# Closing products of a compressed attention branch: high and low parts of two heads stacked over 128 rows

## The chip, the cores and the metric

The kernel runs on one core of one Trainium2 chip. The metric is the device time of one execution in microseconds. The kernel before took 806.31 us, the median of 3 runs (806.19 to 806.38).

## What is computed

One layer of a decoder trunk on 512 tokens of 1024 features, in float32: a normalised input is projected once to queries, keys, values and gates; three attention branches are mixed by gates; a gated short convolution is merged with them; and a feed-forward block with a squared ReLU ends the layer. The change lies in the first of the three branches, attention over compressed keys. Cut to that:

```python
kc = rms_norm(compress(k_c, cmp_pos_k, w_cmp_k), k_norm_g[0])   # 31 compressed keys, 2 groups
vc = compress(v_c, cmp_pos_v, w_cmp_v)                          # and their values
s_c = einsum('bsgrd,bcgd->bgrsc', q, kc) * SCALE - slopes * dist_c
p_c = masked_softmax(s_c, dist_c >= 0)
o_cmp = einsum('bgrsc,bcgd->bsgrd', p_c, vc)
...
o_nsa = g[:, :, 0] * o_cmp + g[:, :, 1] * o_slc + g[:, :, 2] * o_win
```

There are 8 query heads of 64 features in 2 groups (g) of 4 (r); the heads of a group share keys and values. `o_slc` and `o_win` are the two other branches, over selected blocks and over a window, which for 512 tokens are two softmaxes over all earlier tokens.

## The kernel before

**Numbers in two parts.** Float32 operands are split into a high part, which the engine's fast float32 format holds, and a low part, the rest. ACT (ScalarE) writes the high part with a copy, DVE (VectorE) the low part with a subtraction. A product of two matrices is then high by high, high by low and low by high, added in PSUM (`mm3`, L228 to L232). Weights stream from memory in chunks of 128 x 1024 or less (`Weights`): a DMA on SP's queue (L63), ACT's copy to `w_hi` (L87), DVE's subtraction to `w_lo` (L89). A chunk is split one tile ahead of the products that read it.

**Order of the work.** The program writes the order of each engine's instructions out by hand. The outer loop of the stretch that matters is the convolution's (L759): for each of 8 column blocks three tiles of 24 products each (`tile_t`). After every three products `slot` is called; it issues what is due: steps of a background copy of weight sums by DMA (`tick`), short follow-up work put off by some slots (`later`), and one item of a list, `items`, which holds the whole attention, spread evenly over these slots. So attention work sits between the products of the convolution's projections, and each engine executes in the order of issue.

**The attention items.** A unit is a head and one of two branches; 16 units follow each other, two to a head. For unit u the rounds hold: scores for 4 (or 3) token blocks (`u_scores`, L640), each followed on DVE by a bias and maximum (L648), on ACT by the exponential (L652) and on GpSimd (POOL) by the normalisation (L668); transposes of the probabilities of the unit before in three groups (`u_trans`, L687), split by ACT (L692) and DVE (L693) into `pt`; products of the transposed probabilities of the unit before that with V (`u_pv`, L708 and L711), added up in one PSUM tile `pv`. The transposes of L687 and those of L618 take turns in two PSUM buffers (`ps_tr`); the scores have three buffers (`ps_sc`), and `pv` has one.

**The compressed branch** enters `pv` at the end of each head. Its steps:

- `cmp_v` (L477) makes the compressed values, 64 rows (2 groups of 32) by 64 features, splits them into `vcn` (L480, L481) and copies them into `VC` four times each, at rows 0, 32, 64 and 96 (L489, L491), so that each head finds a copy on the rows on which its probabilities lie.
- `cmp_scores` (L580), once for each of the 4 token blocks, writes the scores of the 8 heads side by side (L585), 2 x 32 columns each, adds the distances and forms the softmax in `pcs` (L595 to L610), 32 columns a head in the order of heads, with the slopes of that order from a constant table and the gates of the branch (L609).
- `cmp_pt` (L615), called for g = 0 and g = 1 in two items right after each other and once in the kernel, transposes four heads of one group at once (L618): 128 rows, 32 for each head, by 512 tokens. ACT copies them to the high tile of `pct[g]` (L623), DVE subtracts into the low one (L624).
- `u_fin` (L715), at the end of each head, has two products. The first is over the head's 32 rows of the low part with the high part of the values (64 columns of weights, L722), the second over the 32 rows of the high part with high and low parts of the values (128 columns, L723). ACT and DVE then add the two halves of `pv` into the head's output `oT` (L725, L726).

The same split of one transposed tile in two halves of 64 rows is done for the query heads in `q_item` (L426): two heads are transposed at once, and for each of them ACT copies its 64 rows (L435) and DVE subtracts (L436).

Of the kernel before, what the change touches and what calls it, by code (L numbers as in the profile page):

```python
# [6 lines left out]
F32 = mybir.dt.float32  # L7
F32R = mybir.dt.float32r
AF = mybir.ActivationFunctionType
ALU = mybir.AluOpType  # L10
# [3 lines left out]
P = 128  # L14
S = 512
DM = 1024
NH = 8
HD = 64
# [86 lines left out]
def layer(tc, flat, sizes, x, cst, wck, wcv, g1, g2, out):  # L105
    nc = tc.nc
    top = ExitStack()

    def pool(name, bufs=1, psum=False, side=None, dram=False):
        kw = dict(name=name, bufs=bufs, reuse_waits="tile")  # L110
        if psum:
            kw["space"] = PSUM
        if dram:
            kw["space"] = bass.MemoryType.DRAM
        if side:
            kw["side"] = side
        es = ExitStack()
        p = es.enter_context(tc.tile_pool(**kw))
        return p, es.close
# [48 lines left out]
    ident = cp.tile([P, P], F32, name="ident")  # L168
# [87 lines left out]
    for c in range(NT):  # L256
        ps = ps_acc.tile([P, 512], F32, name="acc", tag="acc")
        for kp in range(4):
            hi, lo = W.get(kp)
# [16 lines left out]
    for c in range(NT):  # L276
        v = q_sb[:, c, :].rearrange("p (h d) -> p h d", d=HD)
# [67 lines left out]
    def later(k, fn):  # L345
        due.append((pos[0] + k, fn))
# [14 lines left out]
    def tile_t(ci, rhs, nko, psp, tag="acc"):  # L361

        ps = psp.tile([P, S], F32, name="acc", tag=tag)
        tile_t_into(ps, ci, rhs, nko)
        return ps
# [42 lines left out]
    ps = tile_t(ci, (xh, xl), NKO, ps_t)  # L408
# [6 lines left out]
    gates = cp.tile([P, NT, 24], F32, name="gates")  # L415
# [4 lines left out]
    QS = [qkv.tile([P, S], F32R, name=f"QS_{h}") for h in range(NH)]  # L420
# [38 lines left out]
    vcn = pre.tile([64, 2, HD], F32R, name="vcn")  # L459
    kc_ss = pre.tile([64, 1], F32, name="kc_ss")  # L460
    KC = qkv.tile([P, 2, 2, 32], F32R, name="KC")
    VC = qkv.tile([P, 2, 2, HD], F32R, name="VC")

    def compress(ps, nm, w):
        for l in range(16):
            src = KAB[nm + "ab"[l // 8]][:, l % 8, :, :].rearrange("p g c -> p (g c)")
            nc.tensor.matmul(ps, src, w[:, l, :], start=(l == 0), stop=(l == 15))
# [9 lines left out]
    def cmp_v():  # L477
        ps = ps_tr.tile([P, S], F32, name="ptr", tag="tr")
        compress(ps[:64, :HD], "v", wcv_t)
        nc.scalar.activation(vcn[:, 0, :], ps[:64, :HD], AF.Copy)  # L480
        nc.vector.tensor_tensor(  # L481
            vcn[:, 1, :], ps[:64, :HD], vcn[:, 0, :].bitcast(F32), ALU.subtract
        )
        for g in range(2):
            for r in range(4):
                dst = VC[32 * r : 32 * r + 32, g, :, :]
                src = vcn[32 * g : 32 * g + 32, :, :].bitcast(F32)
                if r % 2:
                    nc.vector.tensor_copy(dst, src)  # L489
                else:  # L490
                    nc.scalar.activation(dst, src, AF.Copy)  # L491

    def cmp_kt():
        pt = ps_tr.tile([P, 4, P], F32, name="ptr", tag="tr")
# [2 lines left out]
        src = pt[:, 0, :64].rearrange("p (g c) -> p g c", g=2)  # L497
        nc.scalar.activation(KC[:, :, 0, :], src, AF.Copy, scale=sc)
        nc.vector.scalar_tensor_tensor(
            KC[:, :, 1, :], src, sc, KC[:, :, 0, :].bitcast(F32), op0=ALU.mult, op1=ALU.subtract  # L500
        )
# [30 lines left out]
    for c in range(NT):  # L532
        r = k_ss[:, c, :].unsqueeze(2).to_broadcast([P, 4, HD])
        nc.vector.tensor_tensor(kn[:, c, :, 1, :], kn[:, c, :, 0, :], r, ALU.mult)
        nc.gpsimd.tensor_tensor(kn[:, c, :, 0, :], kn[:, c, :, 0, :], r, ALU.mult)
    ps = tile_t(ci, (xh, xl), NKO, ps_t)
# [3 lines left out]
    for i in range(4):  # L540
        items.append((p0 + 18 + 2 * i, lambda i=i: k_item(i)))
    items.append(kt)
    items.append((p0 + 29, cmp_v))

    acc = kv_gemm(ci)
# [14 lines left out]
    ps_pv, close_ps_pv = pool("ps_pv", 1, psum=True, side="left")  # L560
    ap, close_ap = pool("att")
    pcs = [ap.tile([P, NH, 32], F32, name=f"pc{c}") for c in range(NT)]
    pct = [[ap.tile([P, S], F32R, name=f"pct{g}{i}") for i in range(2)] for g in range(2)]
    pbuf = [
        [ap.tile([P, P * (c + 1)], F32, name=f"p{b}_{c}") for c in range(1, NT)] for b in range(2)
    ]
# [13 lines left out]
    def cmp_scores(c):  # L580
        t = slice(c * P, (c + 1) * P)
        ps = ps_sc.tile([P, NH, 2, 32], F32, name="scc", tag="sc")
        for h in range(NH):
            g = h // 4
            nc.tensor.matmul(  # L585
                ps[:, h, :, :], QS[h][:, t], KC[:, g, :, :].rearrange("p a c -> p (a c)"),
                start=True, stop=True,
            )
        pc = pcs[c]
        s = cst_s[:, c, :]  # L590
        dc = cs[:, C_DC + 32 * c : C_DC + 32 * c + 32].unsqueeze(1).to_broadcast([P, NH, 32])
        mk = cs[:, C_MK + 32 * c : C_MK + 32 * c + 32].unsqueeze(1).to_broadcast([P, NH, 32])
        sl = cs[:, C_SL : C_SL + NH].unsqueeze(2).to_broadcast([P, NH, 32])
        sb = s.unsqueeze(2).to_broadcast([P, NH, 32])
        nc.vector.tensor_tensor(pc, ps[:, :, 0, :], dc, ALU.add)  # L595
        nc.vector.tensor_tensor(pc, ps[:, :, 1, :], pc, ALU.add)
        nc.vector.tensor_reduce(s, pc, AX.X, ALU.max)
        nc.gpsimd.tensor_tensor(pc, pc, sb, ALU.subtract)
        nc.gpsimd.tensor_tensor(pc, pc, sl, ALU.mult)

        def second():
            nc.scalar.activation(pc, pc, AF.Exp)
            nc.gpsimd.tensor_tensor(pc, pc, mk, ALU.mult)

        def third():
            nc.vector.tensor_reduce(s, pc, AX.X, ALU.add)
            nc.vector.tensor_scalar(s, s, 1.0e-30, None, op0=ALU.max)
            nc.vector.reciprocal(s, s)
            nc.vector.tensor_tensor(s, s, gates[:, c, 0:NH], ALU.mult)  # L609
            nc.gpsimd.tensor_tensor(pc, pc, sb, ALU.mult)  # L610

        later(3, second)
        later(6, third)

    def cmp_pt(g):  # L615
        pt = ps_tr.tile([P, 4, P], F32, name="ptr", tag="tr")
        for c in range(NT):
            nc.tensor.transpose(  # L618
                pt[:, c, :], pcs[c][:, 4 * g : 4 * g + 4, :].rearrange("p r c -> p (r c)"), ident
            )  # L620
        flat_pt = pt.rearrange("p c t -> p (c t)")
        hi, lo = pct[g]
        nc.scalar.activation(hi, flat_pt, AF.Copy)  # L623
        nc.vector.tensor_tensor(lo, flat_pt, hi.bitcast(F32), ALU.subtract)  # L624


    units = [(h, br) for h in range(NH) for br in range(2)]
# [87 lines left out]
    def u_fin(u):  # L715
        h = units[u][0]
        g, r = h // 4, h % 4
        pv = pv_now[0]
        rr = slice(32 * r, 32 * r + 32)
        v = VC[rr, g, :, :].rearrange("p a d -> p (a d)")  # L720
        chi, clo = pct[g]
        nc.tensor.matmul(pv[:HD, :], v[:, :HD], clo[rr, :], start=False, stop=False)  # L722
        nc.tensor.matmul(pv, v, chi[rr, :], start=False, stop=True)  # L723
        o = oT[(h % 2) * HD : (h % 2 + 1) * HD, h // 2, :]
        nc.scalar.activation(o, pv[HD:, :], AF.Copy)  # L725
        nc.vector.tensor_tensor(o, pv[:HD, :], o, ALU.add)  # L726
# [4 lines left out]
    for u in range(nu + 2):  # L731
        s = [lambda c=c, u=u: u_scores(u, c) for c in (3, 2, 1, 0)[: 4 - u % 2]] if u < nu else []
        t, f = [], []
        if 1 <= u <= nu:
            t = [lambda g=g, v=u - 1: u_trans(v, g) for g in ((3, 2), (1,), (0,))]
        if u >= 2:
            f = [lambda j=j, v=u - 2: u_pv(v, j) for j in ((0, 1), (2, 3))]
# [65 lines left out]
    for n in range(NKO):  # L803
        sg = []
        for i in range(2):
            ps = tile_t(ci, (xh, xl), NKO, ps_t)
            s = gp.tile([P, S], F32, name=f"sg{i}", tag=f"sg{i}")
# [9 lines left out]
        ps = tile_t(ci, (oh, ol), 4, ps_t)  # L817
        nc.vector.tensor_tensor(sg[0], ps, sg[0], ALU.mult)
        ps = tile_t(ci + 1, (zh, zl), NKO, ps_t)
# [4 lines left out]
        if n == 0:  # L824

            r = [t[:, k : k + 2, :].rearrange("p a t -> p (a t)") for t, k in
                 ((z, 0), (z, 2), (z, 4), (z, 6), (oT, 0), (oT, 2))]
# [412 lines left out]
def _constants():  # L1240

    import numpy as np

    f = np.float32
    h = np.arange(NH)
    qs = np.broadcast_to(2.0 ** (h - 2.0), (P, NH)).astype(f)
    sl = np.broadcast_to(2.0 ** -(h + 1.0), (P, NH)).astype(f)
    p = np.arange(P)[:, None]
    c = np.arange(S)[None, :]
    dist = p - (c - 384)  # L1250
    dd = np.where(dist >= 0, -dist, NEG).astype(f)
    dist = p - c % P + c // P * P
    dr = np.where(dist >= 0, -dist, NEG).astype(f)
    t = np.arange(NT)[None, :, None] * P + np.arange(P)[:, None, None]
    cb = np.arange(32)[None, None, :]
    dist = t - (cb * 16 + 31)
    ok = (dist >= 0) & (cb < 31)
    dc = np.where(ok, -dist, NEG).astype(f).reshape(P, -1)
    mk = ok.astype(f).reshape(P, -1)
    return qs, sl, np.eye(P, dtype=f), dd, dr, dc, mk  # L1260
# [41 lines left out]
```

## Time and profile before

| | |
|---|---|
| median of 3 runs | 806.31 us |
| the profiled execution's own time | 806.49 us |
| its span, first to last instruction | 804.6 us |
| granted TensorE clock | 1.0 in every row |
| products on PE (TensorE) | 4421 |
| closing products of the branch, L722 and L723 | 8 each, 128.5 to 275.5 us |
| splits of the transposed probabilities, L623 and L624 | 2 each, 126.1 to 128.6 us |

PE is TensorE's products and PEld its weight loads, which run beside the products. Rows of single instructions give start, duration, engine, line, operation, output and inputs, then shapes; in brackets stands the idle time of the engine just before it and what ended it. Matmuls are pipelined: a row's duration is from its start to its modelled end, and the next one starts before that. For products "128*64" says how many rows and columns of the array are used, so "32*64" is a product over 32 rows.

### The profile page before, as it was taken

The numbers are of one execution on the slowest core, as the hardware profiler recorded it, in microseconds if no ns is written. First come the engines' busy times: TensorE is split into PE (matmuls) and PEld (weight loads), VectorE is DVE, ScalarE is ACT, GpSimd is POOL, SyncE is SP. The second block draws the span as 40 slices with busy tenths as digits, with TensorE's granted clock in tenths as the row PEclk, the third lists the DMA queues.
The fourth block names the chain that finished last, engine by engine and source line by source line (L and its number), as shares of the span: only waits on it lengthen the run. The fifth ranks groups of instructions, "written<-read, shape, count | busy, mean of one in ns | idle before, by whom it ended". The sixth has DMA issues, their size and how long they took to land.

```text
span 804.6 us, 11911 instructions
## 1 busy us (share of the span) xinstructions
PE 786.8 (98%) x4421; PEld 678.1 (84%) x4421; DVE 583.4 (73%) x1005; ACT 394.2 (49%) x714; POOL 88.5 (11%) x138
## 2 busy tenths in 40 slices
PE   5999999999999999999999999899999999999998
PEld 4898877888888788888888789887998899889987
DVE  6578787666666456656665668898699679957984
ACT  5545645545555452233223356973465356545641
POOL 0011563224322300000000000000000000000000
PEclk9999999999999999999999999999999999999999
DMA  9346578567856758998999933649998985555562
GB/s 342 119 138 197 161 159 184 183 153 170 202 158 125 178 117 291 314 323 328 338 333 328 357 105 105 200 148 282 266 267 252 264 262 187 195 192 183 185 208 79
DMA packets 49450, 172.56 MB, mean 214 GB/s; under 512 B 5616, under 2 KB 6000, under 8 KB 49392
## 3 DMA queue, kind: packets, MB, share of 16 engines
q1 hardware_dynamic: 42768, 148.14, 53.7%
q0 software_dynamic: 4608, 16.78, 13.7%
q10 hardware_dynamic: 2016, 6.88, 2.4%
q8 instruction: 35, 0.57, 0.3%
q14 instruction: 23, 0.19, 0.1%
HBM read 152.90 MB, written 52.43 MB: 255 GB/s over the span
## 4 chain that ended last, share of the span: by engine, by line
PE 88%; ACT 4%; DVE 3%; DMA 2%; issue 2%; POOL 0%; SPq 0%; ACTq 0%; DVEq 0%; POOLq 0%
PE acc L230 16%; PE acc L232 15%; PE acc L231 15%; PE dacc L230 6%; PE dacc L231 6%; PE dacc L232 5%; PE uacc L230 4%; PE uacc L232 4%; PE uacc L231 4%; PE sc L640 2%; PE ptu L687 2%; PE uz L232 2%; PE uz L230 2%; PE uz L231 2%; ACT w_hi L87 1%
## 5 line engine op out<-in xcount | busy, mean ns | idle before, releaser
L89 DVE TENSOR_TENSOR w_lo<-w_raw,w_hi 128x512 fp32r<-128x512 f32 (+3 forms) x268 | 233.2, 885 | 75.3 <-ACT w_hi L87 75.1
L87 ACT ACTIVATE w_hi<-w_raw 128x512 fp32r<-128x512 f32 (+3 forms) x268 | 201.2, 778 | 93.1 <-PE dacc L232 63.0
L230 PE MATMUL acc<-xh,w_hi 128*128 128x512 f32 x336 | 137.5, 409 | 0.0
L232 PE MATMUL acc<-xh,w_lo 128*128 128x512 f32 x336 | 131.7, 392 | 0.0
L231 PE MATMUL acc<-xl,w_hi 128*128 128x512 f32 x336 | 131.1, 390 | 0.0
L230 PE MATMUL dacc<-w_hi,uh 128*128 128x512 f32 (+1 forms) x228 | 88.0, 386 | 1.0 <-DVE x L1131 1.0
L231 PE MATMUL dacc<-w_lo,uh 128*128 128x512 f32 (+1 forms) x228 | 88.0, 386 | 0.0
L232 PE MATMUL dacc<-w_hi,ul 128*128 128x512 f32 (+1 forms) x228 | 87.9, 385 | 0.0
L232 PEld LDWEIGHTS acc<-xh,w_lo 128*128 128x128 f32 x336 | 63.0, 188 | 14.3
L230 PEld LDWEIGHTS acc<-xh,w_hi 128*128 128x128 f32 x336 | 63.2, 188 | 11.8 <-issue 3.2
L231 PEld LDWEIGHTS acc<-xl,w_hi 128*128 128x128 f32 x336 | 63.3, 188 | 7.9
L230 PE MATMUL uacc<-hA,w_hi 128*128 128x256 f32 x192 | 54.5, 284 | 0.8 <-ACT w_hi L87 0.8
L652 ACT ACTIVATE p<-p,nst 128x512 f32<-128x512 f32 (+2 forms) x48 | 29.5, 615 | 51.1 <-DVE nst L648 49.9
L232 PE MATMUL uacc<-hA,w_lo 128*128 128x256 f32 x192 | 54.3, 283 | 0.0
L231 PE MATMUL uacc<-hA,w_hi 128*128 128x256 f32 x192 | 54.3, 283 | 0.0
L230 PEld LDWEIGHTS dacc<-w_hi,uh 128*128 128x128 f32 x228 | 42.9, 188 | 10.0 <-ACT w_hi L87 1.4
L232 PEld LDWEIGHTS dacc<-w_hi,ul 128*128 128x128 f32 x228 | 42.8, 188 | 8.6
L231 PEld LDWEIGHTS dacc<-w_lo,uh 128*128 128x128 f32 x228 | 42.8, 188 | 8.5 <-DVE w_lo L89 0.2
L1131 DVE TENSOR_TENSOR x<-x,dacc 128x512 f32<-128x512 f32 (+1 forms) x57 | 36.7, 671 | 9.8 <-PE dacc L232 9.8
L693 DVE TENSOR_TENSOR pt<-ptu,pt 128x384 fp32r<-128x384 f32 (+1 forms) x48 | 28.8, 599 | 17.6 <-ACT pt L692 17.5
L668 POOL TENSOR_SCALAR p<-p,nst 128x512 f32<-128x512 f32 (+2 forms) x48 | 32.0, 674 | 84.3 <-DVE nst L666 41.6
L295 POOL DMA_DIRECT2D td<-w_flat x8 | 6.5, 842 | 307.9 <-DMA td<-w_flat 307.9
(231 smaller groups left out, 1683.4 us busy)
## 6 DMA issues: line engine op xcount, KB each, us to landing
w_raw<-w_flat SPq DMA_DIRECT2D x110, 512.0 KB, 4.8
w_raw<-tu SPq DMA_DIRECT2D x32, 512.0 KB, 4.7
w_raw<-td SPq DMA_DIRECT2D x32, 512.0 KB, 4.5
tu<-w_flat SPq DMA_DIRECT2D x16, 512.0 KB, 6.3
z<-w_flat SPq DMA_DIRECT2D x16, 512.0 KB, 6.9
tu<-w_flat POOLq DMA_DIRECT2D x8, 512.0 KB, 7.9
tu<-tu POOLq DMA_DIRECT2D x8, 512.0 KB, 8.7
td<-w_flat SPq DMA_DIRECT2D x8, 512.0 KB, 5.9
```

Source lines behind the costliest of these rows:

```text
L87: nc.scalar.activation(hi[:, v], t[:, v], AF.Copy)
L89: nc.vector.tensor_tensor(lo[:, v], t[:, v], hi[:, v].bitcast(F32), ALU.subtract)
L230: nc.tensor.matmul(ps, a[0], b[0], start=start, stop=False, **kw)
L231: nc.tensor.matmul(ps, a[0], b[1], start=False, stop=False, **kw)
L232: nc.tensor.matmul(ps, a[1], b[0], start=False, stop=stop, **kw)
L295: nc.gpsimd.dma_start(h[k], h[m], accum_op=ALU.add)
L640: nc.tensor.matmul(ps[:, : b - a], QS[h][:, t], ks[h // 4][:, a:b], start=k == 0, stop=k == 1)
L652: later(1, lambda: nc.scalar.activation(p, p, AF.Exp, scale=-1.0, bias=mn, accum_out=sm))
L668: nc.gpsimd.tensor_scalar(p_of(u, k), p_of(u, k), nst[:, u % 4, 1, k : k + 1], 1.0, op0=ALU.mult, op1=ALU.mult,)
L687: nc.tensor.transpose(pt[:, n : n + P], p_of(u, c)[:, k * P : (k + 1) * P], ident)
L693: later(1, lambda: nc.vector.tensor_tensor(ptl[:, at], pt[:, :n], pth[:, at].bitcast(F32), ALU.subtract))
L1131: nc.vector.tensor_tensor(v, v, ps[:, o : o + n], op)
```

## The change

The rows are laid out anew so that the high and the low part of one head's probabilities, for both groups, are summed over in one product of 128 rows. The scores of the compressed branch are written with the two groups of the same r next to each other, and the table of slopes and the view of the gates follow that order. `cmp_pt` is called for k = 0 and k = 1 as before and transposes four heads, now r = 2k and r = 2k + 1 of both groups. Each half of 64 rows (one r, both groups) is split by itself: the high part goes to rows 0 to 63 of `pct[r]`, the low part to rows 64 to 127 of it. `VC` holds, for a group g, the values at rows 32g (high and low parts) and at rows 64 + 32g (high part alone, in the first 64 columns); all else is zero, from a memset on POOL early in the kernel. The closing product of a head is then one, over 128 rows and with 128 columns; the rows of the other group meet zeros.

```diff
     VC = qkv.tile([P, 2, 2, HD], F32R, name="VC")
+    nc.gpsimd.memset(VC.bitcast(F32), 0.0)
...
         for g in range(2):
-            for r in range(4):
-                dst = VC[32 * r : 32 * r + 32, g, :, :]
-                src = vcn[32 * g : 32 * g + 32, :, :].bitcast(F32)
-                if r % 2:
-                    nc.vector.tensor_copy(dst, src)
-                else:
-                    nc.scalar.activation(dst, src, AF.Copy)
+            src = vcn[32 * g : 32 * g + 32, :, :].bitcast(F32)
+            nc.scalar.activation(VC[32 * g : 32 * g + 32, g, :, :], src, AF.Copy)
+            nc.vector.tensor_copy(VC[64 + 32 * g : 96 + 32 * g, g, 0, :], src[:, 0, :])
...
-    pct = [[ap.tile([P, S], F32R, name=f"pct{g}{i}") for i in range(2)] for g in range(2)]
+    pct = [ap.tile([P, S], F32R, name=f"pct{r}") for r in range(4)]
...
             nc.tensor.matmul(
-                ps[:, h, :, :], QS[h][:, t], KC[:, g, :, :].rearrange("p a c -> p (a c)"),
+                ps[:, 2 * (h % 4) + g, :, :], QS[h][:, t], KC[:, g, :, :].rearrange("p a c -> p (a c)"),
...
-            nc.vector.tensor_tensor(s, s, gates[:, c, 0:NH], ALU.mult)
+            s_ = s.rearrange("p (r g) -> p r g", g=2)
+            gt = gates[:, c, 0:NH].rearrange("p (g r) -> p r g", g=2)
+            nc.vector.tensor_tensor(s_, s_, gt, ALU.mult)
...
-        hi, lo = pct[g]
-        nc.scalar.activation(hi, flat_pt, AF.Copy)
-        nc.vector.tensor_tensor(lo, flat_pt, hi.bitcast(F32), ALU.subtract)
+        for i in range(2):
+            src, to = flat_pt[64 * i : 64 * i + 64], pct[2 * k + i]
+            nc.scalar.activation(to[:64], src, AF.Copy)
+            nc.vector.tensor_tensor(to[64:], src, to[:64].bitcast(F32), ALU.subtract)
...
-        rr = slice(32 * r, 32 * r + 32)
-        v = VC[rr, g, :, :].rearrange("p a d -> p (a d)")
-        chi, clo = pct[g]
-        nc.tensor.matmul(pv[:HD, :], v[:, :HD], clo[rr, :], start=False, stop=False)
-        nc.tensor.matmul(pv, v, chi[rr, :], start=False, stop=True)
+        v = VC[:, g, :, :].rearrange("p a d -> p (a d)")
+        nc.tensor.matmul(pv, v, pct[r], start=False, stop=True)
...
-    sl = np.broadcast_to(2.0 ** -(h + 1.0), (P, NH)).astype(f)
+    sl = np.broadcast_to(2.0 ** -(h // 2 + h % 2 * 4 + 1.0), (P, NH)).astype(f)
```

More of the change, by code (lines that the diff above doesn't have):

```diff
@@ L613, in cmp_scores, with cmp_pt @@
         later(6, third)
-    def cmp_pt(g):
+    def cmp_pt(k):
         pt = ps_tr.tile([P, 4, P], F32, name="ptr", tag="tr")
@@ L618, in cmp_pt @@
             nc.tensor.transpose(
-                pt[:, c, :], pcs[c][:, 4 * g : 4 * g + 4, :].rearrange("p r c -> p (r c)"), ident
+                pt[:, c, :],
+                pcs[c][:, 4 * k : 4 * k + 4, :].rearrange("p r c -> p (r c)"),
+                ident,
             )
         flat_pt = pt.rearrange("p c t -> p (c t)")
-        hi, lo = pct[g]
-        nc.scalar.activation(hi, flat_pt, AF.Copy)
-        nc.vector.tensor_tensor(lo, flat_pt, hi.bitcast(F32), ALU.subtract)
+        for i in range(2):
+            src, to = flat_pt[64 * i : 64 * i + 64], pct[2 * k + i]
+            nc.scalar.activation(to[:64], src, AF.Copy)
+            nc.vector.tensor_tensor(to[64:], src, to[:64].bitcast(F32), ALU.subtract)
     units = [(h, br) for h in range(NH) for br in range(2)]
```

## The prediction

> **What bounds the kernel now.** I read the page first, then three long stretches of the span, then the waits of TensorE (PE), and at the end single stretches instruction by instruction. From the page:
>
> ```profile
> span 804.6 us, 11911 instructions
> ...
> PE 786.8 (98%) x4421; PEld 678.1 (84%) x4421; DVE 583.4 (73%) x1005; ACT 394.2 (49%) x714; POOL 88.5 (11%) x138
> ...
> PE 88%; ACT 4%; DVE 3%; DMA 2%; issue 2%; POOL 0%; SPq 0%; ACTq 0%; DVEq 0%; POOLq 0%
> ```
>
> PE is busy for 98% of the span and is 88% of the chain that ended last; no other engine is near. That is an average, so the stretches come next: the attention stage beside the convolution's projections (130 to 282 us), what lies between it and 470 us, and the rest. The columns are length, then busy us and instructions of PE, PEld, DVE, ACT, POOL, then granted clock, DMA share, GB/s.
>
> ```profile
> 130.00:282.00 152.00, 152.00 (x776) 123.39 (x775) 100.10 (x277) 77.17 (x188) 46.13 (x70) 1.00 0.69 172
> 282.00:470.00 188.00, 188.00 (x827) 154.55 (x827) 114.83 (x164) 61.67 (x122) 0.00 (x0) 1.00 0.86 297
> 470.00:804.60 334.60, 328.02 (x2106) 297.97 (x2104) 270.92 (x331) 186.64 (x236) 6.47 (x8) 1.00 0.64 200
> ```
>
> The change lies in the first stretch. PE has no idle time there and DVE is busy for 66% of it, so what PE is spared there should move everything behind it forward: 282 to 470 us is PE without a gap too, and the weight loads and background copies are issued by the program's own count of products, so they move along. Since a busy PE may still be slowed, I looked at when each product starts. Near the end of the stage:
>
> ```profile
> 272.21 0.39 PE L232 MATMUL acc<-xh,w_lo 128*128 128x512 f32 x1
> 272.44 0.39 PE L708 MATMUL pv<-pt,V 128*128 128x512 f32 x1
> 272.67 0.39 PE L711 MATMUL pv<-pt,V 128*64 128x512 f32 x1
> ...
> 273.24 0.39 PE L230 MATMUL acc<-xh,w_hi 128*128 128x512 f32 x1
> 273.47 0.40 PE L231 MATMUL acc<-xl,w_hi 128*128 128x512 f32 x1
> ...
> 274.86 0.40 PE L232 MATMUL acc<-xh,w_lo 128*128 128x512 f32 x1
> 275.19 0.44 PE L722 MATMUL pv<-pct,VC 32*64 32x512 f32 x1
> 275.47 0.39 PE L723 MATMUL pv<-pct,VC 32*128 32x512 f32 x1
> 275.79 0.50 PE L230 MATMUL acc<-xh,w_hi 128*128 128x512 f32 x1
> 276.13 0.39 PE L231 MATMUL acc<-xl,w_hi 128*128 128x512 f32 x1
> ```
>
> A 512-column product over 128 rows lasts 0.39 us but follows its predecessor after 0.23 us, and that step is what it costs. Around the two 32-row products the steps are 0.33, 0.28, 0.32 and 0.34. The waits of the weight loads (waiting line, us in total, times, longest) say:
>
> ```profile
> PEld acc L230 <- issue: 3.2, 9, 0.4
> PEld pv L722 <- issue: 2.9, 8, 0.4
> ```
>
> The weight load of L722 started only after 0.36 us of idle time, in all 8 places and with nothing of another engine to wait for, and so did the load of the L230 behind the pair (8 of its 9): loads of full products run ahead under the product before, these didn't.
>
> **The products (the gain).** From the start of the last product before the pair (274.86) to the second product behind it (276.13) are 1.27 us. Afterwards the same stretch holds three steps between full products, 3 x 0.23 = 0.69 us: L708 and L711 above are such full products into the same pv. That spares 0.58 us a head, over 8 heads 4.64 us. Bounds: one step alone, 8 x 0.23 = 1.84 us, if the gaps around the product stayed; the 4.64 us if they go. I take 4.64, since all the neighbours with 128 rows, 64 columns wide ones among them, have the plain step.
>
> The row to hold against a rule is the step of 0.28 us between the two 32-row products. The Trainium skill (TensorE: Matmul & The Clock Gate, section Why this matters for your kernels) says that one product over 32 rows takes as long as one over 128 and that the gain of small ones is in running several side by side on different rows; by that alone the sum would be the 1.84 us. Its other page, TensorEngine Tiling (Array Packing), section Key Properties, says that a change of tiling mode drains TensorE, by which the sum would be the 4.64 us; the idle 0.36 us ahead of L722 agrees with the second.
>
> **The transposed probabilities (the cost).** One split of four heads becomes two splits of 64 rows, each an ACT copy and a DVE subtraction. Half the rows spare nothing:
>
> ```profile
> L725 ACT ACTIVATE oT<-pv x8: 592/594/597, 129.2 to 275.9; 64x512 f32<-64x512 f32 x8
> L726 DVE TENSOR_TENSOR oT<-pv,oT x8: 682/683/684, 129.9 to 276.5; 64x512 f32<-64x512 f32 x8
> ```
>
> against 0.60 and 0.69 us for 128 rows:
>
> ```profile
> 126.12 0.60 ACT L623 ACTIVATE pct<-ptr 128x512 fp32r<-128x512 f32 x1 [1.71 <-PE ptr L618]
> 126.75 0.69 DVE L624 TENSOR_TENSOR pct<-ptr,pct 128x512 fp32r<-128x512 f32 x1 [0.94 <-ACT pct L623]
> 127.26 0.60 ACT L623 ACTIVATE pct<-ptr 128x512 fp32r<-128x512 f32 x1 [0.54 <-PE ptr L618]
> 127.89 0.69 DVE L624 TENSOR_TENSOR pct<-ptr,pct 128x512 fp32r<-128x512 f32 x1 [0.45 <-ACT pct L623]
> 128.50 0.68 DVE L89 TENSOR_TENSOR w_lo<-w_raw,w_hi 128x512 fp32r<-128x512 f32 x1
> ```
>
> So ACT gets 1.2 us more and DVE 1.37 us. Whether two splits of one transposed tile overlap is seen at the query heads, which already split one tile in two halves of 64 rows:
>
> ```profile
> 44.71 0.68 ACT L435 ACTIVATE QS<-ptr,gq 64x512 fp32r<-64x512 f32 x1 [4.40 <-PE ptr L429]
> 45.42 0.74 DVE L436 SCALAR_TENSOR_TENSOR QS<-ptr,gq,QS 64x512 fp32r<-64x512 f32 x1 [0.37 <-ACT QS L435]
> 46.20 0.68 ACT L435 ACTIVATE QS<-ptr,gq 64x512 fp32r<-64x512 f32 x1 [0.81 <-DVE QS L436]
> ```
>
> The second ACT copy waits for the first DVE subtraction. With that alternation, a copy taking 0.60, a subtraction 0.69 and the hand-over 0.04 us, the first pair runs from 126.12 to 127.44 and the second to 128.80. The third copy is of the other tile and needs only ACT (128.08 to 128.68), so its subtraction follows at once and ends at 129.48; the fourth copy waits for that, and the last subtraction ends at 130.84, where before it ended at 128.58. DVE is then 2.26 us late (with no alternation 127.44 + 3 x 0.68 = 129.48, 0.9 us late). The first closing product needs only the first pair, ready at 127.44, about a microsecond before its turn. Behind the late subtraction queue L89 (a weight split, for a chunk that PE reaches a tile later), then L726 and the next scores' softmax. What could reach PE is the pair of transpose buffers:
>
> ```profile
> 132.14 0.49 PE L687 MATMUL ptu<-ident,p 128*128 128x128 f32 x3
> 133.74 0.56 DVE L693 TENSOR_TENSOR pt<-ptu,pt 128x384 fp32r<-128x384 f32 x1 [0.69 <-ACT pt L692]
> 136.76 0.27 PE L687 MATMUL ptu<-ident,pz 128*128 128x128 f32 x1
> 137.90 0.39 PE L708 MATMUL pv<-pt,V 128*128 128x512 f32 x1
> 138.65 0.69 DVE L693 TENSOR_TENSOR pt<-ptu,pt 128x512 fp32r<-128x512 f32 x1 [1.22 <-ACT pt L692]
> 141.90 0.69 DVE L648 CUSTOM_DVE_ANT_0 p<-sc,cs 128x512 f32<-128x512 f32 x1 [1.49 <-PE sc L640]
> ```
>
> The transposes of 136.76 take the buffer of those of 132.14, which L693 frees at 134.30, or 136.56 if late by 2.26; PE, 0.58 us earlier, wants it at 136.18. Cost 0.4 us, once. If the pairs overlap it is nothing; if no slack helped, 2.26 us. I take 0.4. The next pv tile (137.90, or 137.3) waits for L726, which would end near 132.8: covered. The idle 1.22 and 1.49 us let DVE catch up within one round.
>
> **The values of the compressed keys.** Eight copies become four, and a memset is added:
>
> ```profile
> L489 DVE CAST VC<-vcn x4: 217/218/220, 81.9 to 82.6; 32x128 fp32r<-32x128 f32 x4
> L491 ACT ACTIVATE VC<-vcn x4: 307/308/309, 81.9 to 82.8; 32x128 fp32r<-32x128 f32 x4
> L574 POOL MEMSET pt<- x4: 204/204/206, 81.4 to 83.3; 128x128 f32 x4
> 64.16 2.93 POOL L535 TENSOR_TENSOR kn<-kn,k_ss 128x256 f32<-128x256 f32 x4 [20.90 <-DVE kn L534]
> ```
>
> ACT loses 0.62 us and DVE at least 0.44 us while PE works on; worth 0 to 0.6 us, and I take 0, as PE waits for neither there. The memset has twice L574's columns, 0.41 us at most, and POOL's queue has 20.9 us of idle time ahead of L535; uncovered it would cost 0.4 us. Other order of heads in the scores, slopes and gates: the same instructions on other columns, nothing (at the most 0.1 us in each of four small DVE products).
>
> **Sum.** 4.64 - 0.4 = 4.2 us. The profiled execution took 806.49 us, which gives 802.3; the median of the runs is 806.31 us, and from it the forecast is 802.1 us.
>
> **The rivals.** No change smaller than about 0.2% (1.6 us) can be told from none here.
> Overlapping splits: the framework may let ACT read one half while DVE reads the other. For it: they are different partitions; against it, L435. 806.31 - 4.64 = 801.7 us, with the 0.6 us of the copies 801.1. Chance 0.20.
> One step only: the gaps stay, because a wait or the accumulation into pv makes them and not the 32 rows. Against it: L708 and L711 accumulate into pv without gaps. 806.31 - 1.84 = 804.5 us. Chance 0.08.
> DVE late by its full 2.26 us on PE's path: the splits are slower than taken or the lag meets a second buffer. 806.31 - 4.64 + 2.26 = 803.9 us. Chance 0.12.
> The gain runs into a transfer later: the last stretch leaves PE idle for 334.60 - 328.02 = 6.6 us, part of which might be fixed in time. But the transfers are issued by PE's progress. 806.3 us. Chance 0.06.
> Slower: the attention rounds are bound by the chain through DVE and ACT, and PE only looks busy. Then sparing PE brings nothing and the 2.26 us of added alternation lie on the path: 808.6 us. It decides if DVE cannot work off the lag within the rounds up to 282 us. For it: PE did wait for DVE earlier in the attention stage,
>
> ```profile
> PE ptu L687 <- DVE pt L693: 0.9, 2, 0.6
> ```
> ```profile
> 121.67 0.30 PE L687 MATMUL ptu<-ident,pz 128*128 128x128 f32 x1 [0.30 <-DVE pt L693]
> ```
>
> against it: 66% of DVE, and that this, the second of the two, was the last. Chance 0.04.
>
> **How the numbers follow.** The forecast, 802.1, has 0.50. The range, 801.0 to 804.2 us, takes in it, the overlapping splits and the late DVE, 0.82 together; outside are one step only, no gain and slower (0.18). Faster by over 0.2%, below 804.7 us: 0.50 + 0.20 + 0.12 + most of 0.08 = 0.89; within 0.2%: 0.07; slower: 0.04.
>
> **What would show it.** PE's products fall from 4421 to 4413, ACT and DVE keep their counts, POOL has one more. The closing product should start 0.23 us behind its predecessor in all eight places, with no idle weight load, and the steps behind it should be 0.23. The four copies of pct on ACT should alternate with the subtractions, the last ending near 130.8 us; the transposes near 136.2 us wait about 0.4 us for L693's counterpart. PE's end of the stage comes 4.2 us sooner and so does the end. I am wrong if the gap ahead of the product stays, or if PE waits for DVE in later rounds.

## The result and the profile after

The changed kernel took 801.88 us (median of 5 runs, 800.82 to 802.44) against 806.21 us of the kernel before (5 runs, 804.48 to 806.38): a ratio of 0.9944, with a 95% interval of 0.9934 to 0.9955. The profiled execution took 802.44 us, 4.05 us less than the one of before.

The page of the changed kernel:

```profile
span 800.7 us, 11895 instructions
...
PE 782.3 (98%) x4413; PEld 678.0 (85%) x4413; DVE 584.0 (73%) x1005; ACT 394.6 (49%) x714; POOL 89.6 (11%) x139
...
PE 85%; DVE 6%; ACT 5%; DMA 2%; issue 2%; POOL 0%; SPq 0%; ACTq 0%; DVEq 0%; POOLq 0%
```

PE has eight products less, ACT and DVE have as many instructions as before, POOL has the memset more, and the chain that ended last is still PE's for the most part. Two of the three stretches of the prediction, in the same times (length, busy us and instructions of PE, PEld, DVE, ACT and POOL, granted clock, DMA share, GB/s):

```profile
130.00:282.00 152.00, 151.65 (x784) 126.29 (x783) 102.85 (x283) 77.34 (x189) 46.87 (x70) 1.00 0.71 175
282.00:470.00 188.00, 188.00 (x829) 154.54 (x828) 116.85 (x166) 65.33 (x130) 0.00 (x0) 1.00 0.84 294
```

PE, which had no idle time in the first, now has 0.35 us there. At the last head the steps from one product's start to the next were 0.33, 0.28, 0.32 and 0.34 us before. The same place now (L725 is the closing product):

```profile
270.88 0.39 PE L232 MATMUL acc<-xh,w_lo 128*128 128x512 f32 x1
270.88 0.19 PEld L725 LDWEIGHTS pv<-pct,VC 128*128 128x128 f32 x1
271.11 0.39 PE L725 MATMUL pv<-pct,VC 128*128 128x512 f32 x1
...
271.35 0.40 PE L230 MATMUL acc<-xh,w_hi 128*128 128x512 f32 x1
271.58 0.39 PE L231 MATMUL acc<-xl,w_hi 128*128 128x512 f32 x1
```

The weights of L725 load while the product before it runs, and all steps are 0.23 us: 0.70 us from 270.88 to 271.58, where it was 1.27. The waits of the weight loads no longer name the closing product, and L230 keeps one of its nine:

```profile
PEld acc L230 <- issue: 0.3, 1, 0.3
```

The splits of the transposed probabilities (L628 on ACT, L629 on DVE; "x2" merges two in a row):

```profile
125.61 0.59 ACT L628 ACTIVATE pct<-ptr 64x512 fp32r<-64x512 f32 x1 [1.71 <-PE ptr L620]
126.95 1.21 ACT L628 ACTIVATE pct<-ptr 64x512 fp32r<-64x512 f32 x2 [0.75 <-DVE pct L629]
129.03 0.60 ACT L628 ACTIVATE pct<-ptr 64x512 fp32r<-64x512 f32 x1 [0.86 <-DVE pct L629]
```
```profile
129.65 0.69 DVE L629 TENSOR_TENSOR pct<-ptr,pct 64x512 fp32r<-64x512 f32 x1 [0.66 <-ACT pct L628]
```

ACT waits for DVE before the second and the fourth copy: they alternate. The last subtraction ends at 130.34. Then, in order, DVE's subtraction of the first group of transposes (L698, L693 before) and PE's third group (L692, L687 before):

```profile
135.49 0.56 DVE L698 TENSOR_TENSOR pt<-ptu,pt 128x384 fp32r<-128x384 f32 x1 [0.69 <-ACT pt L697]
136.19 0.30 PE L692 MATMUL ptu<-ident,pz 128*128 128x128 f32 x1 [0.35 <-DVE pt L698]
```

PE waits for that subtraction. Of the three waits of this kind in the changed kernel this one is new, the two others (0.9 us together) stood in the kernel before too:

```profile
PE ptu L692 <- DVE pt L698: 1.3, 3, 0.6
```

**Where the time went.** The L230 products, 1268 in each trace, are the marks by which the two traces are laid side by side. The stretch from the last L230 ahead of the first closing product to the second behind the last one is, before and after:

```profile
127.76 0.40 PE L230 MATMUL acc<-xh,w_hi 128*128 128x512 f32 x1
...
276.60 0.39 PE L230 MATMUL acc<-xh,w_hi 128*128 128x512 f32 x1
```
```profile
127.25 0.40 PE L230 MATMUL acc<-xh,w_hi 128*128 128x512 f32 x1
...
272.04 0.39 PE L230 MATMUL acc<-xh,w_hi 128*128 128x512 f32 x1
```

That is 148.84 and 144.79 us, 4.05 us less. Outside it, the stretches between the same products agree within 0.1 us in all ten profiles of this study, but for two places that vary with no regard to the kernel. One is the products before 18 us, whose start depends on the first loads (16.5 to 17.9 us for the sixth L230). The other is one step behind 555 us, 0.78 to 2.46 us long. There a chunk of weights comes late by DMA (`w_raw<-td`, for which ACT waits), DVE's split of it is late in turn, and behind that split stands the addition L1133, for which PE waits. In the changed kernel's first profile this step is the 2.46 us, with a wait of PE of 1.62:

```profile
554.80 1.06 ACT L87 ACTIVATE w_hi<-w_raw 128x1024 fp32r<-128x1024 f32 x1 [5.61 <-DMA w_raw<-td]
...
557.86 0.47 PE L230 MATMUL dacc<-w_hi,uh 128*128 128x512 f32 x1 [1.62 <-DVE x L1133]
```

Below, the stretch of 148.84 us is called the stage, and kernels are compared by it; it was 144.79, 144.78 and 144.77 us in three profiles of the changed kernel.

### The profile page after: what moved, and what is told of

It is laid out like the page before. It is cut to its first block, busy times and chain, and to the rows that moved or that the text cites. A ratio compares the mean times of both kernels' runs of the same rounds, so it can differ in the third digit from the quotient of the medians.

```text
span 800.7 us, 11895 instructions
## 1 busy us (share of the span) xinstructions
PE 782.3 (98%) x4413; PEld 678.0 (85%) x4413; DVE 584.0 (73%) x1005; ACT 394.6 (49%) x714; POOL 89.6 (11%) x139
## 4 chain that ended last, share of the span: by engine, by line
PE 85%; DVE 6%; ACT 5%; DMA 2%; issue 2%; POOL 0%; SPq 0%; ACTq 0%; DVEq 0%; POOLq 0%
PE acc L230 15%; PE acc L232 15%; PE acc L231 15%; PE dacc L230 6%; PE dacc L231 6%; PE dacc L232 6%; PE uacc L230 4%; PE uacc L232 4%; PE uacc L231 4%; PE ptu L692 2%; PE sc L645 2%; PE uz L230 2%; PE uz L232 2%; PE uz L231 2%; DMA w_raw<-td 1%
## 5 line engine op out<-in xcount | busy, mean ns | idle before, releaser
L230 PE MATMUL acc<-xh,w_hi 128*128 128x512 f32 x336 | 136.7, 407 | 0.0
L230 PE MATMUL dacc<-w_hi,uh 128*128 128x512 f32 (+1 forms) x228 | 88.0, 386 | 1.6 <-DVE x L1133 1.6
L230 PEld LDWEIGHTS acc<-xh,w_hi 128*128 128x128 f32 x336 | 63.2, 188 | 9.3 <-issue 0.3
L230 PE MATMUL uacc<-hA,w_hi 128*128 128x256 f32 x192 | 54.5, 284 | 0.7 <-ACT w_hi L87 0.7
L230 PEld LDWEIGHTS dacc<-w_hi,uh 128*128 128x128 f32 x228 | 42.8, 188 | 10.4 <-ACT w_hi L87 2.0
L1133 DVE TENSOR_TENSOR x<-x,dacc 128x512 f32<-128x512 f32 (+1 forms) x57 | 36.7, 672 | 9.8 <-PE dacc L232 9.8
L698 DVE TENSOR_TENSOR pt<-ptu,pt 128x384 fp32r<-128x384 f32 (+1 forms) x48 | 28.8, 600 | 17.8 <-ACT pt L697 17.8
```

The source lines that it names most:

```text
L230: nc.tensor.matmul(ps, a[0], b[0], start=start, stop=False, **kw)
L698: later(1, lambda: nc.vector.tensor_tensor(ptl[:, at], pt[:, :n], pth[:, at].bitcast(F32), ALU.subtract))
L1133: nc.vector.tensor_tensor(v, v, ps[:, o : o + n], op)
```

## Experiments

The experiments ran in two groups of four kernels, each beside the kernel before, which had medians of 806.53 us (20 runs) and 806.07 us (21 runs). The first group is the changed kernel again and the three with a zero product; the other four are the second.

| kernel | median us (runs) | ratio to before, 95% | stage us |
|---|---|---|---|
| before | 806.53 (20), 806.07 (21) | | 148.84 |
| changed, again | 801.81 (4) | 0.9923 to 0.9954 | 144.78 |
| changed, third | 802.42 (5) | 0.9934 to 0.9962 | 144.77 |
| with a zero product over 32 rows | 806.80 (10) | 0.9991 to 1.0010 | 149.24 |
| with a zero product over 64 rows | 806.61 (10) | 0.9987 to 1.0008 | 149.17 |
| with a zero product over 128 rows | 804.57 (5) | 0.9955 to 0.9984 | 146.40 |
| before, one product over 32 rows | 804.73 (10) | 0.9973 to 0.9991 | 147.36 |
| splits reordered | 801.75 (5) | 0.9927 to 0.9952 | 144.25 |
| subtractions doubled | 807.12 (10) | 0.9998 to 1.0016 | 149.22 |

My theory was the prediction's: most of the gain is the round trip, from products over 128 rows to one over fewer rows and back. The rivals: the number of products, or two products into the same rows.

**The changed kernel again**, no edit, in the first and in the second group.

> The changed kernel once more, to compare the next three with on one chip. 801 to 802.5 us; the transposes behind the splits wait 0.35 us for DVE again, since that wait is made by the alternation of ACT and DVE and not by chance.

> The changed kernel again, beside the reordered one on one chip: 801 to 802.5 us, with the wait of 0.35 us for DVE at the third group of transposes.

801.81 and 802.42 us, and the wait of PE for L698 is 0.34 us in both traces, against 0.35 in the first.

**A zero product of 32, 64 or 128 rows ahead of the closing one.** `ptb`, the buffer of the transposed probabilities `pt`, holds a block of 128 x 128 zeros from a memset; as weights they add nothing to the result.

```diff
+        zero = ptb[u % 2][1][:32, :P]
+        nc.tensor.matmul(pv, zero, pct[r][:32], start=False, stop=False)
         nc.tensor.matmul(pv, v, pct[r], start=False, stop=True)
```

> A product over 32 rows with zero weights is added ahead of each closing product (it adds zeros). Theory, the change of the row count makes PE wait for the products before to be through, on the way in and on the way out: steps of 0.33, 0.32 and 0.34 in place of 0.23 each, so 0.53 us a head and 4.2 us more than the changed kernel, near 806 us. Rival, a product costs one step whatever its rows, and the gaps of before came from accumulating two products of one head or from waits: 0.23 us a head, 1.8 us more, near 803.7 us.

> The same over 64 rows. Theory, any row count other than that of the neighbours makes PE wait: 4.2 us more than the changed kernel. Rival, only 32 rows do: 1.8 us more.

> The same over 128 rows, so two products a head as before the change, but both of full height. Theory and rival: one step of 0.23 us a head, 1.8 us more than the changed kernel, near 803.7 us. If instead the number of products were what brought the gain, it would be all gone: 806 us.

With 32 rows, at the last head:

```profile
274.69 0.40 PE L232 MATMUL acc<-xh,w_lo 128*128 128x512 f32 x1
275.01 0.18 PEld L726 LDWEIGHTS pv<-pct,pt 32*128 32x128 f32 x1 [0.36 <-issue]
275.01 0.49 PE L726 MATMUL pv<-pct,pt 32*128 32x512 f32 x1
275.43 0.19 PEld L727 LDWEIGHTS pv<-pct,VC 128*128 128x128 f32 x1 [0.24 <-issue]
275.43 0.50 PE L727 MATMUL pv<-pct,VC 128*128 128x512 f32 x1
...
275.78 0.40 PE L230 MATMUL acc<-xh,w_hi 128*128 128x512 f32 x1
```

and with 128 rows:

```profile
273.45 0.39 PE L232 MATMUL acc<-xh,w_lo 128*128 128x512 f32 x1
273.45 0.19 PEld L726 LDWEIGHTS pv<-pct,pt 128*128 128x128 f32 x1
273.69 0.39 PE L726 MATMUL pv<-pct,pt 128*128 128x512 f32 x1
...
273.91 0.39 PE L727 MATMUL pv<-pct,VC 128*128 128x512 f32 x1
...
274.14 0.40 PE L230 MATMUL acc<-xh,w_hi 128*128 128x512 f32 x1
```

The 32 rows give steps of 0.32, 0.42 and 0.35, in all 0.40 us beyond three plain steps; the weight load idles before the product of 32 rows and again before the one of 128 that follows. The 64 rows give the same, steps of 0.33, 0.42 and 0.34:

```profile
274.84 0.40 PE L232 MATMUL acc<-xh,w_lo 128*128 128x512 f32 x1
...
275.17 0.49 PE L726 MATMUL pv<-pct,pt 64*128 64x512 f32 x1
...
275.59 0.50 PE L727 MATMUL pv<-pct,VC 128*128 128x512 f32 x1
...
275.93 0.39 PE L230 MATMUL acc<-xh,w_hi 128*128 128x512 f32 x1
```

The 128 rows add a plain step each. So the theory holds for 32 and 64 rows: both are back at the time of before. My number was too low. I had taken the step behind the product as 0.32, and it is 0.42, which makes 5.0 us over 8 heads in place of 4.2. The medians differ by 5.0 us, the stages by 4.46: PE now comes later to the third group of transposes and no longer waits for DVE there. Why the step is 0.42 is not shown. The 128 columns of that product alone don't make it, since L723 of the kernel before, with as many columns behind another product over 32 rows, has 0.32 behind it. The 128 rows were to add 1.8 us; the stage grew by 1.62 us against the changed kernel (PE comes later to the wait for DVE and waits about 0.2 us less), the medians by 2.8 us with runs that spread over nearly 2 us.

**One product over 32 rows.** The kernel before without L722; it leaves the low part of these probabilities out.

```diff
-        nc.tensor.matmul(pv[:HD, :], v[:, :HD], clo[rr, :], start=False, stop=False)
         nc.tensor.matmul(pv, v, chi[rr, :], start=False, stop=True)
```

> The kernel before without the first of its two closing products (the low part of the compressed probabilities is left out). Theory, the loss lies in going to 32 rows and back, once a head, whatever the number of products there: 0.28 us a head less at the most, so 804.0 to 805.1 us, and the gaps ahead of the product and behind it stay. Rival, the second product into the same rows makes the gap: it goes, and the time is that of the changed kernel, 801.8 us.

```profile
151.11 0.40 PE L232 MATMUL acc<-xh,w_lo 128*128 128x512 f32 x1
151.44 0.50 PE L722 MATMUL pv<-pct,VC 32*128 32x512 f32 x1
151.86 0.50 PE L230 MATMUL acc<-xh,w_hi 128*128 128x512 f32 x1
152.20 0.40 PE L231 MATMUL acc<-xl,w_hi 128*128 128x512 f32 x1
```

The gaps stay, 0.33, 0.42 and 0.34 us. Half of the closing products are gone, yet the stage lost only 1.48 us, 0.185 a head; the rival is out. A round trip costs 0.40 us beyond the plain steps with one product in it, and 1.27 - 4 x 0.23 = 0.35 us with two. It is paid once a trip, not once a product.

**The splits reordered.** First halves of both tiles, then the second halves.

```diff
-        for i in range(2):
+        def half(i):
             ...
+        half(0)
+        halves.append(lambda: half(1))
+        if k:
+            for f in halves:
+                f()
```

> The changed kernel with the four splits in another order: first half of the first tile, first half of the second tile, then the second halves, so that ACT copies from one tile while DVE reads the other. Theory, the wait of 0.35 us at the third group of transposes comes from the alternation of ACT and DVE on one tile: the splits end 0.7 to 1.0 us sooner, that wait is gone, PE is 0.35 us sooner from there on. Rival, the wait comes from DVE's two additional subtractions alone: it stays. In time 801.5 against 801.8 us, which a timing can hardly tell apart; the trace can.

ACT's rows, then DVE's, in this kernel, which started 1.42 us later than the first profile of the changed one:

```profile
127.03 0.59 ACT L630 ACTIVATE pct<-ptr 64x512 fp32r<-64x512 f32 x1 [1.72 <-PE ptr L622]
128.16 1.93 ACT L630 ACTIVATE pct<-ptr 64x512 fp32r<-64x512 f32 x3 [0.54 <-PE ptr L622]
```
```profile
128.79 2.04 DVE L631 TENSOR_TENSOR pct<-ptr,pct 64x512 fp32r<-64x512 f32 x3 [0.45 <-ACT pct L630]
```

No copy waits for DVE any more; the last subtraction ends at 130.83, which is 129.41 in the times of the first profile, 0.9 us sooner. PE doesn't wait at the third group, which starts one plain step behind its predecessor:

```profile
136.87 0.39 PE L232 MATMUL acc<-xh,w_lo 128*128 128x512 f32 x1
137.10 0.27 PE L700 MATMUL ptu<-ident,pz 128*128 128x128 f32 x1
```

The stage is 144.25 us, 0.53 us shorter than with the alternation. That is more than the 0.35 us of idle time, which count from the modelled end of a product: from start to start, L692 came 0.51 us later than a plain step. The order of the splits was the cause, the work itself is the same. This is the best version by the stage, and it can't be told from the changed kernel by a timing (801.75 and 802.42 us, with spreads of 2.1 and 1.1 us).

**The subtractions doubled.**

```diff
             nc.vector.tensor_tensor(to[64:], src, to[:64].bitcast(F32), ALU.subtract)
+            nc.vector.tensor_tensor(to[64:], src, to[:64].bitcast(F32), ALU.subtract)
```

> The changed kernel with each of the four subtractions of the split done twice (the second writes the same values again). Theory, the lag of DVE reaches PE through the transpose buffers and beyond its cover counts in full: the last subtraction ends 2.7 us later and the wait at the third group of transposes grows from 0.35 to about 3 us, 804.5 us. Rival, DVE has a third of its time free there and works it off: 802 us.

```profile
133.76 0.69 DVE L630 TENSOR_TENSOR pct<-ptr,pct 64x512 fp32r<-64x512 f32 x1
```
```profile
137.21 0.50 PE L646 MATMUL sc<-KS,QS 128*128 128x256 f32 x2 [1.10 <-DVE nst L654]
...
140.29 0.30 PE L693 MATMUL ptu<-ident,pz 128*128 128x128 f32 x1 [1.88 <-DVE pt L699]
...
140.67 0.48 PE L230 MATMUL acc<-xh,w_hi 128*128 128x512 f32 x1
...
142.88 0.63 PE L230 MATMUL acc<-xh,w_hi 128*128 128x512 f32 x1
143.31 0.63 PE L231 MATMUL acc<-xl,w_hi 128*128 128x512 f32 x1
...
144.99 0.39 PE L230 MATMUL acc<-xh,w_hi 128*128 128x512 f32 x1
```

The last subtraction ends at 134.45; this kernel started 1.21 us later than the first profile of the changed one, so DVE is 2.9 us later than there. The rival, that DVE works the lag off, is out: the stage is 4.43 us longer than the changed kernel's. The theory's 804.5 us was too low all the same, by 2.6 us. Waits make about 2.8 us of the 4.43, near the theory's sum, though not where it had them: 1.26 us fall at a score, and at the third group 1.53 us more than in the changed kernel. The rest was in no theory: from 141.81 us the products of 512 columns follow each other at 0.43 us. The granted clock (the number behind the engines) in slices of one microsecond:

```profile
140.00:141.00 1.00, 0.71 (x6) 0.70 (x7) 0.93 (x7) 0.55 (x3) 0.00 (x0) 1.00 0.77 295
...
142.00:143.00 1.00, 1.00 (x5) 0.81 (x4) 1.00 (x5) 0.00 (x0) 0.84 (x1) 0.50 0.67 258
...
145.00:146.00 1.00, 1.00 (x7) 0.83 (x6) 0.93 (x5) 0.50 (x1) 0.18 (x1) 1.00 0.21 86
```

After two idle times of 1.10 and 1.88 us the clock was halved for some 3.4 us, from 141.52 to 144.93 us. From the L230 at 140.67 to that at 144.99 passed 4.32 us, for which the changed kernel took 2.74: 1.58 us lost. The halving doesn't come in every execution: of the ten runs of this kernel, eight had a mean granted clock of 0.995 to 0.998 and took 806.86 to 807.83 us, and two had 1.0, so no such halving, and took 806.20 and 806.54 us.

## Why the prediction was right

**The products.** 4.64 us were forecast. The reordered kernel, in which PE doesn't wait for the splits, has a stage of 144.25 us against 148.84: 4.59 us. Of these, 8 x 0.23 = 1.84 us are the second product and the rest the round trip, 0.35 us a head. That the row count makes it, which I read from the idle 0.36 us ahead of a weight load without a releaser, is shown by the zero products: 32 and 64 rows pay it, 128 don't. What PE does in that time no row shows. The Trainium skill's rule (TensorEngine Tiling (Array Packing), section Key Properties), that a change of tiling mode drains TensorE, agrees, if a mode is a row count: L708 and L711 differ in columns, 128 and 64, and have the plain step.

**The splits.** The alternation came as the query heads' rows had it, and the lag of 2.26 us with it: the last subtraction was to end at 130.84 and ended at 130.34 in an execution that was 0.50 us ahead there (its transposes of this step started at 124.98 in place of 125.48). The wait was where I had put it. Its size was a little off: L698 ended at 136.05 and PE, which would have started at 135.68, did at 136.19, so 0.51 us in place of 0.4. I had let PE start at the end of the subtraction and left out the hand-over of 0.14 us.

**The values and the memset** lay beside other work, as forecast. The memset took 0.30 us in place of the 0.41 I had allowed:

```profile
42.67 0.30 POOL L464 MEMSET VC<- 128x256 f32 x1
```

**The sum** was 4.2 us; the stage gave 4.05 us, of which nothing was lost later by the change. The end came 4.0 us sooner in the profiled execution, since it also began 0.5 us sooner and its late chunk behind 555 us cost 0.6 us more than in the profile of before. That the median of 801.88 us lies within 0.3 us of the forecast is partly luck: the medians before and after differ by 4.33 us here, and by 4.72 and 3.65 us in the two groups of experiments. I had named a late transfer as a rival; there is one, but it varies by 1.7 us among executions of all these kernels and takes no fixed part of the gain.

**The slower rival**, that DVE and ACT bound the rounds, was wrong for this kernel but not far from a real limit: 2.9 us more of lag in one place, with DVE busy for two thirds of the stage, took away the whole gain in the profiled execution (a stage of 149.22 us), 2.8 us of it by waits and 1.6 by the clock.

## What to carry to other kernels

Look at the steps from start to start, not at durations: the small products lasted 0.44 and 0.39 us like any other, and only the starts about them showed that 1.27 us passed where four plain steps take 0.92. A product over fewer rows among full ones is worth filling up with zeros, or at least gathering with others of its kind, since the trip was paid once for one product and for two. When one engine copies from a PSUM tile and another reads the same tile, give them two tiles to take turns on.

## What the runs showed of the hardware

A product over 64 rows is as dear as one over 32: steps of 0.33, 0.42 and 0.34 us about it. And in the profiled execution with the subtractions doubled, an idle time of 1.88 us, with 1.10 us of another shortly before, was followed by a halved granted clock for some 3.4 us, which cost 1.6 us on top of the waits; two of the ten runs of that kernel went without it. The stretches at one clock last 126.293, 3.413 and 662.186 us in that trace, which is 37, 1 and 194 times 3.413. If the clock is set anew every 3.413 us, as these lengths suggest, the last such stretch ahead of the halving, 138.10 to 141.52 us, held the wait of 1.88 us alone. That is an inference; no run here puts the wait elsewhere. In the changed kernel the wait of 1.62 us behind 555 us had no such sequel:

```profile
558.00:560.00 2.00, 2.00 (x10) 1.64 (x11) 2.00 (x3) 0.73 (x1) 0.00 (x0) 1.00 0.94 330
```

The Trainium skill (TensorE: Matmul & The Clock Gate, section Why this matters for your kernels) asks for no idle gaps above some 3 us. In that profiled execution less in one piece came before the halving.
